# Two-directional state-space scan in a mixer kernel: step sizes in the exponents, decays added ahead of the scores, token-major inner sum, norm factors in the output weights, state chain by head

## The chip, the cores and the metric

One NeuronCore of one Trainium2 chip runs the whole program: both layers of the trunk, all 768 tokens. The metric is the device time of one execution in microseconds; the median of several executions is compared. Every time below is in microseconds unless it is marked ns. Engines are written as in the profile: PE (TensorE), DVE (VectorE), ACT (ScalarE), POOL (GpSimd) and SP (SyncE, whose queue issues most transfers).

## The reference

A trunk of two layers over 512 latent tokens and 256 context tokens (width 1024). Each layer has one input projection whose columns feed two groups of heads: a gated depthwise convolution with LayerNorm, and a state-space scan in both directions. Their outputs are concatenated, multiplied by `w_out` and added to the tokens; a mixture of experts (MoE) follows. The change touches the scan and the norm behind it:

```python
SSD_HEADDIM = 64; SSD_HEADS = 8; SSD_GROUPS = 2; SSD_STATE = 128; SSD_CHUNK = 128

def ssd_chunked(xs, dt, a, bm, cm, h0):      # one direction
    a_cum = jnp.cumsum((dt * a).reshape(b, nc, SSD_CHUNK, nh), axis=2)
    xdt = (xs * dt[..., None]).reshape(b, nc, SSD_CHUNK, nh, hp)
    causal = jnp.tril(jnp.ones((SSD_CHUNK, SSD_CHUNK), dtype=bool))
    seg = a_cum[:, :, :, None, :] - a_cum[:, :, None, :, :]
    decay_ls = jnp.exp(jnp.where(causal[None, None, :, :, None], seg, -jnp.inf))
    scores = jnp.einsum("bclhn,bcshn->bclsh", cc, bc) * decay_ls
    y_diag = jnp.einsum("bclsh,bcshp->bclhp", scores, xdt)
    decay_to_end = jnp.exp(a_cum[:, :, -1:, :] - a_cum)
    chunk_states = jnp.einsum("bclh,bclhn,bclhp->bchpn", decay_to_end, bc, xdt)
    chunk_decay = jnp.exp(a_cum[:, :, -1, :])
    # h_prev: scan over chunks of  h * chunk_decay + chunk_states
    y_off = jnp.einsum("bclhn,bchpn,bclh->bclhp", cc, h_prev, jnp.exp(a_cum))
    return (y_diag + y_off).reshape(b, l, nh, hp)

def mixer_output(...):
    y = y_f + y_b + p["d_skip"][:, None] * xs
    ssd_out = rms_norm(y.reshape(b, l, D_SSD) * jax.nn.silu(z), p["ssd_norm_g"])
    return jnp.concatenate([conv_out, ssd_out], axis=-1) @ p["w_out"]
```

## The kernel before

The tokens are cut into chunks of 128: chunks 0 to 3 are latent, 4 and 5 context. Layer 0 scans all six; layer 1, the last, needs only the latent four, but forms the states of all. A chunk lies with its tokens on the 128 partitions, so a 128x512 tile is one chunk of all eight heads. The arithmetic of this part is fp32. `xs` and `zs` (the scan's input and its gate) are the two halves of the tile `bigA`.

The mixer of a layer runs through four stages that overlap:

1. The input projection. `xbc_tile` (line 814) makes the columns of x, B and C, one tile of 128 columns at a time, with a short convolution as five DVE instructions (lines 830 and 832); `decays` (line 792) makes the step sizes' cumulated decays, writes their transposed sums to DRAM as `cumd`, and keeps the factors `ex` and the negative sums `ncum`.
2. The states. For each chunk POOL multiplies `xs` by both directions' factors (line 936), PE turns B (line 939), DVE copies it (line 941), PE forms two 128x512 states (line 947), ACT and DVE copy them from PSUM into `wraw` or `tab` (line 949). Then the chain: four steps in each direction, a state times its decay plus the next state (line 959 on DVE, line 960 on DVE or, for the backward direction, on POOL), through a temporary of the pool `Y`. The last columns of C, the chunks of z and the LayerNorm of the convolution (`ln_steps`, line 881, with the square root at line 364 on POOL and the multiply at line 906 on DVE) run beside it.
3. The scan, chunk by chunk. `prep` (line 971) reads a chunk's row of `cumd` to all partitions for each direction (line 975), masks it on POOL (line 977) and takes eight exponentials on ACT (line 980), into one of two pairs of decay buffers `E`. `scores` (line 982) forms C times B on PE (line 986) and C times the incoming states (line 993), multiplies both directions' decays by the scores on DVE (line 997), scales `xs` by both directions' step sizes on POOL (line 998) and starts `Y` with the skip term (line 1000) and the states' part (lines 1003 and 1004). `inside` (line 1007) sums both directions over the chunk with 32 matmuls whose result stands channel by token (line 1013), copies it from PSUM (line 1016), turns it back with four transposes (line 1019), adds it and multiplies by z (lines 1020 and 1021), and takes the RMS norm with the gain `sng` (lines 1023 and 1025). `turn_y` (line 1027) turns `Y` again for the output projection (lines 1030, 1033, 1034).
4. The output projection. One unit is two chunks times 256 columns: 48 matmuls (lines 491 to 493). Layer 0 has 12 units, layer 1 has 8. The first ones stand between chunks of the scan, the others follow it; `out_weights` (line 1042) loads `w_out` and splits it in two parts (lines 1059 and 1060).

The loop over chunks writes `prep` of chunk c+1 ahead of `inside` of chunk c; the decays of chunk c+2 use the buffers of chunk c. Within that, the order of instructions on each engine is set by a scheduler that simulates a timeline when the program is built; an engine then works strictly in that order. Pools bound it: eight buffers for `t4`, three for `Y`, two for `t2` and `wp`, two PSUM buffers each for `sm`, `tp` and `mm`. The MoE behind each mixer streams its weights into the buffers that the mixer frees.

```python
for c in order:
    Ys[c] = scores(c)
    if c < order[-1]:
        prep(c + 1)
    if units:
        out_proj(*units.pop(0))
    if c:
        turn_y(c - 1, Ys[c - 1])
        residual(c - 1)
    inside(c, Ys[c])
```

## Time and profile before

| what | us |
|---|---|
| median of three executions (1306.15 to 1311.55) | 1311.16 |
| the profiled execution, its own time | 1300.17 |
| its span | 1298.5 |
| busy in it: PE / DVE / ACT / POOL | 1100.1 / 784.1 / 550.7 / 570.7 |
| scan and end of output projection, layer 0 | about 331 to 461 |
| scan and end of output projection, layer 1 | about 958 to 1052 |

The profile is of one execution, 10.99 us below the median. PE is busy in 85% of the span, but the share of each stage differs, so the stages are read one by one: a view with busy times by stretch, then the timeline of the engines in it. In a timeline a group of like instructions in a row is one line with its count; the bracket at its end is the idle time ahead of it on its engine and what released it. In the view by stretch each engine has its busy time and the number of its instructions, then come the granted TensorE clock (1.00 is full speed), the busy share of the DMA engines and GB/s.

### The profile page before, as it was taken

To read this page: it belongs to the slowest core of one execution; us is meant where nothing else is said; L and a number is where in the kernel's file an instruction comes from. 1 tells how busy PE (TensorE), PEld (TensorE's weight loads), DVE (VectorE), ACT (ScalarE), POOL (GpSimd) and SP (SyncE) were. 2 spreads that over 40 slices of the span, in tenths; PEclk is the share of its full clock that TensorE was granted. 3 is DMA by queue.
4 is the path that set the end of the run, shared out by engine and by line. 5 is a ranking of instruction groups with operands and counts; after the bars stand their busy time and mean duration, and the time that the engine had idled before them with its cause. 6 is when DMAs were issued, how large, how long until landed. Compare 5 with 4: busy or idle time off the path is not lost. (4 is left out here: it accounts for less than half of the span.)

```text
span 1298.5 us, 20274 instructions
## 1 busy us (share of the span) xinstructions
PE 1100.1 (85%) x7595; PEld 915.6 (71%) x7595; DVE 784.1 (60%) x1199; ACT 550.7 (42%) x976; POOL 570.7 (44%) x445
## 2 busy tenths in 40 slices
...
DMA packets 113810, 261.18 MB, mean 201 GB/s; under 512 B 16033, under 2 KB 53519, under 8 KB 108589
## 3 DMA queue, kind: packets, MB, share of 16 engines
...
q8 instruction: 61, 1.00, 0.3%
...
## 5 line engine op out<-in xcount | busy, mean ns | idle before, releaser
L474 POOL TENSOR_TENSOR t<-wp,t 128x1024 fp32r<-128x1024 f32 (+1 forms) x36 | 99.2, 2760 | 192.2 <-ACT t L473 187.1
L491 PE MATMUL mm<-t,HL 128*128 128x256 f32 (+1 forms) x448 | 133.3, 298 | 8.0 <-DVE acc L906 4.0
L493 PE MATMUL mm<-t,HL 128*128 128x256 f32 (+1 forms) x448 | 130.4, 291 | 1.1 <-DVE HL L1034 1.1
L492 PE MATMUL mm<-t,HL 128*128 128x256 f32 (+1 forms) x448 | 130.1, 290 | 0.0
L1461 POOL DMA_INDIRECT acc_d<-t,idx x38 | 70.5, 1856 | 77.7 <-ACT t L1456 24.9
L1376 POOL TENSOR_TENSOR C<-raw,wraw 128x1024 fp32r<-128x1024 f32 x28 | 78.4, 2850 | 58.9 <-PE sm L493 39.6
L491 PEld LDWEIGHTS mm<-t,HL 128*128 128x128 f32 x448 | 87.9, 196 | 17.6 <-issue 6.5
L493 PEld LDWEIGHTS mm<-t,HL 128*128 128x128 f32 x448 | 87.6, 196 | 5.4 <-issue 3.7
L492 PEld LDWEIGHTS mm<-t,HL 128*128 128x128 f32 x448 | 87.9, 196 | 4.9 <-issue 4.8
L832 DVE SCALAR_TENSOR_TENSOR t<-t,pcol,t 128x772 f32<-128x772 f32 (+1 forms) x64 | 87.8, 1372 | 2.1
L492 PE MATMUL sm<-C,t 128*128 128x256 f32 (+8 forms) x304 | 85.7, 282 | 3.9 <-DVE C L1376 3.9
L491 PE MATMUL mm<-HL,t 128*128 128x512 f32 (+1 forms) x224 | 85.0, 380 | 2.8 <-ACT HL L385 1.6
L364 POOL TENSOR_TENSOR rstd<-ms,mhalf 128x1 f32<-128x1 f32 (+3 forms) x29 | 23.0, 796 | 143.9 <-DVE ms L362 143.9
L492 PE MATMUL mm<-HL,t 128*128 128x512 f32 (+1 forms) x224 | 82.8, 370 | 0.0
L493 PE MATMUL mm<-HL,t 128*128 128x512 f32 (+1 forms) x224 | 82.4, 368 | 0.0
L1375 ACT CAST wraw<-raw 128x1024 fp32r<-128x1024 f32 x64 | 66.0, 1048 | 35.8 <-DMA raw<-in_w_down_dram 18.7
L493 PE MATMUL sm<-HL,t 128*128 128x256 f32 (+8 forms) x272 | 77.3, 284 | 1.9 <-DVE t L1406 1.9
L492 PE MATMUL sm<-HL,t 128*128 128x256 f32 (+8 forms) x272 | 76.7, 282 | 2.2 <-DVE HL L1376 2.2
L491 PE MATMUL sm<-HL,t 128*128 128x256 f32 (+8 forms) x272 | 78.3, 288 | 0.1
L473 ACT CAST t<-wp 128x1024 fp32r<-128x1024 f32 (+1 forms) x40 | 41.9, 1056 | 82.8 <-PE mm L492 63.9
L1384 POOL DMA_INDIRECT t<-h2d,idx x38 | 52.8, 1390 | 52.6 <-PE sm L1360 16.6
L1376 POOL TENSOR_TENSOR HL<-raw,HL 128x1024 fp32r<-128x1024 f32 x24 | 61.2, 2603 | 19.9 <-ACT HL L1375 14.8
...
## 6 DMA issues: line engine op xcount, KB each, us to landing
...
raw<-in_w_gate_dram SPq DMA_DIRECT2D x60, 512.0 KB
raw<-in_w_up_dram SPq DMA_DIRECT2D x60, 512.0 KB
raw<-in_w_down_dram SPq DMA_DIRECT2D x60, 512.0 KB
wp<-in_w_in_dram SPq DMA_DIRECT2D x40, 512.0 KB
wp<-in_w_out_dram SPq DMA_DIRECT2D x16, 512.0 KB
...
v<-cumd SPq DMA_DIRECT2D x15, 512.0 KB
```

What stands on the lines that cost most here:

```text
L364: G.tensor_tensor(r[:, :n], ms[:, :n], mhalf[:, :n], op=OP.pow)
L473: S.copy(hi, t)
L474: eng.tensor_sub(lo, t, hi)
L491: T.matmul(dst, lh, rh, start=(k == 0), stop=False)
L492: T.matmul(dst, lh, rl, start=False, stop=False)
L493: T.matmul(dst, ll, rh, start=False, stop=(k == K8 - 1))
L832: V.scalar_tensor_tensor(xa[:, :n], xpt[:, tap:tap + n], col, xa[:, :n], op0=OP.mult, op1=OP.add)
L1375: highs.append(S.copy(hi, r))
L1376: eng.tensor_sub(lo, r, hi)
L1384: gathered.append(G.indirect_dma_start(out=xg[:n], out_offset=None, in_=h2d, in_offset=bass.IndirectOffsetOnAxis(ap=icol[:n], axis=0)))
L1461: G.indirect_dma_start(out=acc_d, out_offset=bass.IndirectOffsetOnAxis(ap=icol[:n], axis=0), in_=y[:n], in_offset=None, compute_op=OP.add)
```

## The change

- **Step sizes in the exponents.** The scores need the decay times dt. The kernel takes ln(dt), floored at 1e-37, adds it to `ncum` and uses the sum `ldt` as the bias of the exponentials. Two DVE instructions and one ACT instruction a layer are new in `decays`; the POOL multiply of `xs` by the step sizes (line 998) goes.
- **Both directions added ahead of the scores.** A POOL addition of 128x1024 joins the two directions' exponentials in `prep`; one DVE multiply by the scores is left of two. The second buffer of a pair is free after the addition.
- **Inner sum token major.** Eight matmuls with the decays of a head as stationary operand and 64 columns of `xs` moving give the result token by channel; the 32 matmuls, the copy and the four transposes go.
- **Norm.** The gain goes into the second half of the output weights, one DVE multiply of 128x1024 for each of four column blocks a layer, from columns of the parameter tile; the load of `sng` becomes a small load at the start. The RMS factor goes into a diagonal matrix (a DVE instruction of 128x128), and `turn_y` multiplies `Y` by it instead of by the identity; line 1025 goes.
- **Chain by head.** Each of the eight steps is eight DVE instructions of 128x64 that multiply and add in one, 64 a layer, in place of eight multiplies on DVE and eight additions on DVE and POOL. The temporary goes.

```diff
--- before.py
+++ after.py
@@ -195,7 +195,7 @@
     dsk = const.tile([P, 2, 8], F32, name="dsk")
     rb = const.tile([P, 2, 2, 20], F32, name="rb")
     wr = const.tile([P, 2, K8, 32], F32, name="wr")
-    pcol = const.tile([P, 120], F32, name="pcol")
+    pcol = const.tile([P, 128], F32, name="pcol")
     cwcol = [const.tile([P, 124], F32, name=f"cwcol{l}") for l in range(2)]
     av = const.tile([P, 2, 16], F32, name="av")
     block0, capv = [const.tile([P, 2, 16], F32, name=n) for n in ("block0", "capv")]
@@ -207,10 +207,11 @@
 
     def params():
         rows = main.tile([P, 4, P], F32, name="ad", bufs=3)
-        prow, cwrow = rows[:120, 0], rows[:124, 1:3]
+        prow, cwrow = rows[:128, 0], rows[:124, 1:3]
         for off, n, src in ((0, 8, conv_b), (8, 8, conv_ln_g), (16, 8, conv_ln_b), (24, 16, ssd_conv_b)):
             nc.sync.dma_start(out=prow[off:off + n, :], in_=src.rearrange("l (k p) -> (l k) p", p=P))
         nc.sync.dma_start(out=prow[40:120, :], in_=ssd_conv_w.rearrange("l t (k p) -> (l t k) p", p=P))
+        nc.sync.dma_start(out=prow[120:128, :], in_=ssd_norm_g.rearrange("l (k p) -> (l k) p", p=P))
         nc.sync.dma_start(out=cwrow, in_=conv_w.rearrange("l t (k p) -> (t k) l p", p=P))
         nc.sync.dma_start(out=dtb.rearrange("p l e -> p (l e)"), in_=bcast(dt_bias, 0, [[0, P], [1, 32]]))
         nc.sync.dma_start(out=alog.rearrange("p l e -> p (l e)"), in_=bcast(a_log, 0, [[0, P], [1, 32]]))
@@ -533,7 +534,7 @@
         vB, vC = [t.rearrange("p a b -> p (a b)").rearrange("p (j t) -> p j t", j=2) for t in (vB, vC)]
         for n, b in (("Y", 3), ("t2", 2)):
             mixp.tile([P, 512], F32, name=n, bufs=b)
-        dtr, dts, dA, ncum = [mixp.tile([P, 2, 6, 8], F32, name=n) for n in ("dtr", "dts", "dA", "ncum")]
+        dtr, dts, dA, ncum, ldt = [mixp.tile([P, 2, 6, 8], F32, name=n) for n in ("dtr", "dts", "dA", "ncum", "ldt")]
         ex = mixp.tile([P, 3, 2, 6, 8], F32, name="ex")
         BT = mixp.tile([P, 2, NT], F32, name="BT")
         CT = mixp.tile([P, 2, NT], F32, name="CT")
@@ -798,6 +799,9 @@
             S.activation(ex.rearrange("p q d c h -> p (q d c h)"), ps[:, :288], AF.Exp)
             V.tensor_mul(ex[:, 1], ex[:, 1], dts)
             V.tensor_scalar(f96(ncum), ps[:, 288:384], -1.0, None, op0=OP.mult)
+            V.tensor_scalar(ldt, dts, 1e-37, None, op0=OP.max)
+            S.activation(ldt, ldt, AF.Ln)
+            V.tensor_add(ldt, ldt, ncum)
             pt = tp_tile()
             T.transpose(pt[0:96, 0:P], f96(ncum), ident)
             cumT = main.tile([P, 512], F32, name="ad", bufs=3)
@@ -920,8 +924,6 @@
             for i in range(7):
                 nc.sync.dma_start(out=acc_d[i * P:(i + 1) * P, :], in_=z)
 
-        sng = main.tile([P, 512], F32, name="ad", bufs=3)
-        nc.sync.dma_start(out=sng, in_=bcast(ssd_norm_g, l * 512, [[0, P], [1, 512]]))
         rooms["held"], rooms["next"] = False, 0
         Sb, Sa, Sc = [wraw_tile([P, 4, 512], F32) for _ in range(3)]
         St = {4: [Sa[:, 0], Sa[:, 1]], 5: [Sa[:, 2], Sa[:, 3]], 1: [Sb[:, 0], Sb[:, 1]],
@@ -955,9 +957,10 @@
         for i in range(1, 5):
             for d in range(2):
                 c0, c1 = chain[d][i - 1], chain[d][i]
-                t = mixp.tile([P, 512], F32, name="Y", bufs=3)
-                V.tensor_mul(hview(t), hview(St[c0][d]), hbc(ex[:, 2], d, c1, 64))
-                (G if d else V).tensor_add(St[c1][d], St[c1][d], t)
+                for h in range(NH):
+                    hs = slice(64 * h, 64 * h + 64)
+                    V.scalar_tensor_tensor(St[c1][d][:, hs], St[c0][d][:, hs], ex[:, 2, d, c1, h:h + 1], St[c1][d][:, hs],
+                                           op0=OP.mult, op1=OP.add)
         ln_fill()
         af(1)
         fill(1)
@@ -977,7 +980,9 @@
                 G.affine_select(out=e, in_=e, pattern=[[0, NH], [(1, -1)[d], P]],
                                 compare_op=OP.is_ge, fill=-1e30, base=0, channel_multiplier=(-1, 1)[d])
                 for h in range(NH):
-                    S.activation(e[:, h, :], e[:, h, :], AF.Exp, bias=ncum[:, d, c, h:h + 1])
+                    S.activation(e[:, h, :], e[:, h, :], AF.Exp, bias=ldt[:, d, c, h:h + 1])
+            e = E[c % 2]
+            G.tensor_add(e[0], e[0], e[1])
 
         def scores(c):
 
@@ -992,10 +997,8 @@
                 for g in range(2):
                     T.matmul(pf[:, d * 512 + g * 256:d * 512 + (g + 1) * 256], CT[:, g, c * P:(c + 1) * P],
                              H[:, g * 256:(g + 1) * 256], start=True, stop=True)
-            for d in range(2):
-                e = E[c % 2][d].rearrange("p (g h) q -> p g h q", g=2)
-                V.tensor_mul(e, e, pq[:, :256].rearrange("p (g q) -> p g q", g=2)[:, :, None, :].to_broadcast([P, 2, 4, P]))
-            G.tensor_mul(v4(xdt), hview(xs[:, c, :])[:, None].to_broadcast([P, 2, NH, 64]), both(dts, c, 64))
+            e = E[c % 2][0].rearrange("p (g h) q -> p g h q", g=2)
+            V.tensor_mul(e, e, pq[:, :256].rearrange("p (g q) -> p g q", g=2)[:, :, None, :].to_broadcast([P, 2, 4, P]))
             Y = mixp.tile([P, 512], F32, name="Y", bufs=3)
             G.tensor_mul(hview(Y), hview(xs[:, c, :]), dsk[:, l, :, None].to_broadcast([P, NH, 64]))
             for i, d in enumerate(dirs):
@@ -1006,28 +1009,23 @@
 
         def inside(c, Y):
 
-            pyT = sm_tile()
-            for h in range(0, NH, 2):
-                for d in range(2):
-                    for j in range(2):
-                        T.matmul(pyT[64 * j:64 * j + 64, h * 64:h * 64 + P], xdt[:, d, (h + j) * 64:(h + j + 1) * 64],
-                                 E[c % 2][d][:, h + j, :], start=(d == 0), stop=(d == 1))
-            yT = t2_tile()
-            (V.tensor_copy if last else S.copy)(yT, pyT)
-            py = tp_tile()
-            for f in range(4):
-                T.transpose(py[:, f * P:(f + 1) * P], yT[:, f * P:(f + 1) * P], ident)
+            py = sm_tile()
+            for h in range(NH):
+                hs = slice(64 * h, 64 * h + 64)
+                T.matmul(py[:, hs], E[c % 2][0][:, h, :], xs[:, c, hs], start=True, stop=True)
             V.tensor_add(Y, Y, py)
             V.tensor_mul(Y, Y, zs[:, c, :])
             ss = sml.tile([P, 8], F32, name="ss")
-            S.activation(yT, Y, AF.Square, accum_out=ss[:, 0:1])
+            S.activation(t2_tile(), Y, AF.Square, accum_out=ss[:, 0:1])
             r = rstd_of(ss, 1, 512.0, RMS_EPS)
-            V.scalar_tensor_tensor(Y, Y, r[:, 0:1], sng, op0=OP.mult, op1=OP.mult)
-
-        def turn_y(c, Y):
+            dg = main.tile([P, P], F32, name="diag", bufs=2)
+            V.tensor_scalar(dg, ident, r[:, 0:1], None, op0=OP.mult)
+            return Y, dg
+
+        def turn_y(c, Y, dg):
             pt = tp_tile()
             for f in range(4):
-                T.transpose(pt[:, f * P:(f + 1) * P], Y[:, f * P:(f + 1) * P], ident)
+                T.matmul(pt[:, f * P:(f + 1) * P], Y[:, f * P:(f + 1) * P], dg, start=True, stop=True)
             p3 = pt.rearrange("p (f t) -> p f t", f=4)
             ks = slice(4, 8)
             S.copy(mh(ks, c * P, (c + 1) * P), p3)
@@ -1048,6 +1046,8 @@
                 raw.append(main.tile([P, 4, 256], F32, name="wp", bufs=2))
                 nc.sync.dma_start(out=raw[h], in_=w_out[l][512 * h:512 * h + 512, 256 * n4:256 * n4 + 256]
                                   .rearrange("(k p) n -> p k n", p=P))
+
+            V.tensor_mul(raw[1], raw[1], pcol[:, 120 + 4 * l:124 + 4 * l, None].to_broadcast([P, 4, 256]))
             for h in range(2):
                 if n4 == 2:
                     hi.append(t2[:, h])
@@ -1092,7 +1092,6 @@
         prep(0)
         split_conv(range(4))
         acc2 = mixp.tile([P, 3, 2, 512], F32, name="acc")
-        xdt = acc2[:, 0]
         ws, units, Ys = {}, [], {}
         for c in order:
             Ys[c] = scores(c)
@@ -1104,14 +1103,14 @@
             if units:
                 out_proj(*units.pop(0))
             if c:
-                turn_y(c - 1, Ys[c - 1])
+                turn_y(c - 1, *Ys[c - 1])
                 residual(c - 1)
-            inside(c, Ys[c])
+            Ys[c] = inside(c, Ys[c])
             if c < 2 or c == 4:
                 ws[min(c, 2)] = out_weights(min(c, 2))
             if c and c % 2 == 0:
                 units += [(n4, ws[n4], c - 2) for n4 in range(2)]
-        turn_y(c, Ys[c])
+        turn_y(c, *Ys[c])
         residual(c)
         for n4 in range(2, 4):
             if n4 not in ws:
```

The scheduler also puts other work in another place. On POOL in layer 0, the three skip terms `Y<-bigA,dsk` stood behind the selects and among the chain's additions:

```order
L977 AFFINE_SELECT v<-v 128x1024
L960 TENSOR_TENSOR wraw<-wraw,Y 128x512
L1000 TENSOR_TENSOR Y<-bigA,dsk 128x512 x2
L960 TENSOR_TENSOR wraw<-wraw,Y 128x512
L1000 TENSOR_TENSOR Y<-bigA,dsk 128x512
L1090 TENSOR_TENSOR HL_2628<-acc,HL_2626 128x512 x2
```

Now they stand ahead of the six multiplies of `xs` that the states begin with (line 936 before, 938 now), as they do in layer 1:

```order
L980 AFFINE_SELECT tab<-tab 128x1024
L899 TENSOR_TENSOR v<-v 128x768 x3
L1003 TENSOR_TENSOR Y<-bigA,dsk 128x512 x3
L938 TENSOR_TENSOR t_2199<-bigA,ex 128x1024
L938 TENSOR_TENSOR t_2214<-bigA,ex 128x1024
```

What moved are the three `Y` instructions, ahead of what the states wait for. On DVE in the same stage of layer 0, before, copies of B from PSUM (`t<-tp`), copies of states (`wraw<-sm`, `tab<-sm`) and the first steps of the chain (lines 959 and 960):

```order
L941 COPY t_2216<-tp 128x256
L959 TENSOR_TENSOR Y<-wraw,ex 128x512
L949 COPY wraw<-sm 128x512
L941 COPY t_2231<-tp 128x256
L960 TENSOR_TENSOR wraw<-wraw,Y 128x512
L949 COPY wraw<-sm 128x512
L941 COPY t_2242<-tp 128x256
L959 TENSOR_TENSOR Y<-wraw,ex 128x512 x2
L941 COPY t_2253<-tp 128x256
L960 TENSOR_TENSOR tab<-tab,Y 128x512
```

and the same place now, with the steps of 64 columns at line 962:

```order
L962 SCALAR_TENSOR_TENSOR wraw<-wraw,ex 128x64 x6
L951 COPY wraw<-sm 128x512
L943 COPY t_2245<-tp 128x256
L962 SCALAR_TENSOR_TENSOR wraw<-wraw,ex 128x64 x2
L943 COPY t_2256<-tp 128x256
L962 SCALAR_TENSOR_TENSOR wraw<-wraw,ex 128x64 x8
L962 SCALAR_TENSOR_TENSOR tab<-wraw,ex,tab 128x64 x7
L951 COPY tab<-sm 128x512
L943 COPY t_2271<-tp 128x256
L962 SCALAR_TENSOR_TENSOR tab<-wraw,ex,tab 128x64
L962 SCALAR_TENSOR_TENSOR wraw<-tab,ex,wraw 128x64 x7
L951 COPY wraw<-sm 128x512
```

Between the copies there now stand 31 short instructions instead of five long ones; 48 of the 64 are ahead of the last copy of a state. On SP's queue in the scan of layer 0, where `v<-cumd` and `tab<-cumd` are the reads for the decays, before:

```order
L975 DMA v<-cumd_1567 128x1024 x3
L1049 DMA wp<-in_w_out_dram 128x4x256 x5
L355 DMA acc<-ada_1059 128x2x512 x2
L1049 DMA wp<-in_w_out_dram 128x4x256
L975 DMA v<-cumd_1567 128x1024 x3
L1065 DMA bigA<-in_x_dram 128x2x512
L975 DMA tab<-cumd_1567 128x1024
```

and now:

```order
L978 DMA v<-cumd_1569 128x1024 x3
L1047 DMA wp<-in_w_out_dram 128x4x256
L978 DMA v<-cumd_1569 128x1024
L978 DMA tab<-cumd_1569 128x1024
L1047 DMA wp<-in_w_out_dram 128x4x256 x2
L356 DMA acc<-ada_1061 128x2x512 x2
L978 DMA v<-cumd_1569 128x1024
L1047 DMA wp<-in_w_out_dram 128x4x256
L978 DMA v<-cumd_1569 128x1024
```

One read for chunk 2 and one for chunk 3 moved ahead of loads of output weights, since the buffer of the second direction is free earlier.

## Rows read from the trace of the kernel before

**Rows 1.** Busy time by stretch, layer 0's and layer 1's state, scan and projection stages.

```profile
285.00:330.00 45.00, 36.29 (x220) 32.88 (x220) 38.16 (x35) 23.53 (x46) 30.84 (x23) 0.85 0.28 84
330.00:390.00 60.00, 44.38 (x395) 38.56 (x394) 45.39 (x53) 33.61 (x90) 46.49 (x33) 0.94 0.50 164
390.00:460.00 70.00, 70.00 (x573) 65.31 (x574) 34.42 (x62) 19.28 (x50) 9.38 (x8) 1.00 0.25 78
...
930.00:958.00 28.00, 24.06 (x164) 18.27 (x162) 25.14 (x23) 20.48 (x39) 20.08 (x15) 0.94 0.73 262
958.00:1020.00 62.00, 50.57 (x411) 42.02 (x407) 46.64 (x57) 24.89 (x56) 37.33 (x25) 0.94 0.66 226
1020.00:1040.00 20.00, 20.00 (x161) 18.68 (x162) 9.22 (x17) 4.87 (x15) 1.71 (x2) 1.00 0.03 10
```

**Rows 2.** Timeline of PE in layer 0's scan, chunks 0 to 2.

```profile
340.00 1.97 PE L1013 MATMUL sm<-v,acc 128*64 128x128 f32 x32 [0.81 <-POOL acc L998]
...
341.89 0.71 PE L986 MATMUL sm<-CT,BT 128*128 128x128 f32 x4
...
342.70 0.66 PE L1019 MATMUL tp<-ident,t 128*128 128x128 f32 x4
...
356.82 1.12 PE L1030 MATMUL tp<-ident,Y 128*128 128x128 f32 x4 [7.66 <-DVE Y L1025]
...
358.72 2.91 PE L1013 MATMUL sm<-v,acc 128*64 128x128 f32 x32
```

**Rows 3.** Timeline of the other engines between `inside` of chunks 0 and 2.

```profile
341.78 5.15 SPq L975 DMA_DIRECT2D v<-cumd  x3
...
349.16 1.28 ACT L980 ACT_TABLE_LOAD   x1 [6.51 <-DMA v<-cumd]
...
350.45 2.44 ACT L980 ACTIVATE v<-v,ncum 128x128 f32<-128x128 f32 x8
...
351.43 1.90 POOL L998 TENSOR_TENSOR acc<-bigA,dts 128x1024 f32<-128x1024 f32 x1
...
352.99 1.22 DVE L997 TENSOR_TENSOR v<-v,sm 128x1024 f32<-128x1024 f32 x1 [5.60 <-ACT v L980]
...
353.28 1.09 POOL L977 TENSOR_SCALAR_AFFINE_SELECT v<-v 128x1024 f32<-128x1024 f32 x1
...
354.96 1.81 DVE L1025 SCALAR_TENSOR_TENSOR Y<-Y,rstd,ad 128x512 f32<-128x512 f32 x1
```

**Rows 4.** Timeline of PE in layer 1's scan, chunks 0 and 2.

```profile
968.48 1.74 PE L1013 MATMUL sm<-v,acc 128*64 128x128 f32 x26
...
988.00 1.75 PE L1013 MATMUL sm<-v,acc 128*64 128x128 f32 x28 [1.39 <-DVE v L997]
```

**Rows 5.** Timeline of POOL and DVE in layer 0's state stage.

```profile
274.25 12.55 POOL L936 TENSOR_TENSOR t<-bigA,ex 128x1024 f32<-128x1024 f32 x6 [1.23 <-ACT bigA L850]
...
277.99 2.42 DVE L959 TENSOR_TENSOR Y<-wraw,ex 128x512 f32<-128x512 f32 x1 [1.69 <-ACT wraw L949]
...
286.75 2.79 POOL L474 TENSOR_TENSOR t<-wp,t 128x1024 fp32r<-128x1024 f32 x1
...
296.14 0.69 DVE L949 COPY wraw<-sm 128x512 f32<-128x512 f32 x1 [2.59 <-PE sm L947]
...
298.38 0.69 DVE L959 TENSOR_TENSOR Y<-wraw,ex 128x512 f32<-128x512 f32 x1
...
298.99 0.68 DVE L959 TENSOR_TENSOR Y<-tab,ex 128x512 f32<-128x512 f32 x1
...
304.51 3.06 POOL L474 TENSOR_TENSOR t<-wp,t 128x1024 fp32r<-128x1024 f32 x1
...
312.81 3.34 DVE L906 TENSOR_TENSOR acc<-acc,mm 128x3072 f32<-128x3072 f32 x1
```

**Rows 6.** One line's forms with least, median and longest ns, first and last start.

```profile
L790 DVE SCALAR_TENSOR_TENSOR acc<-v,cwcol,acc x56: 269/479/2560, 103.6 to 789.1; 128x64 f32<-128x64 f32 x8, 128x128 f32<-128x128 f32 x8, 128x192 f32<-128x192 f32 x8, 128x256 f32<-128x256 f32 x8
```

**Rows 7.** Timeline of ACT around the step sizes of layer 0.

```profile
202.85 0.59 ACT L821 COPY t<-mm 128x512 f32<-128x512 f32 x1 [10.86 <-PE mm L493]
```

## The prediction

> **What bounds the kernel now.** I read the busy times by stretch first, then the timeline of the engines in the scan. In layer 0's scan (330 to 390) no engine is full: PE is busy 44.4 of 60 us, DVE 45.4, POOL 46.5, ACT 33.6. Behind it, from 390 to 460, PE is busy all the time [rows 1]. So the mixer ends when the scan is through and PE has done what is left of the output projection. PE's idle time in the scan is 60 - 44.38 = 15.6 us, and 7.66 of it is one wait, for the normed `Y` of chunk 0 [rows 2]. Behind that stands a loop over the decay buffers. Chunk 2 reuses chunk 0's pair: its reads are issued at 341.78, when `inside` of chunk 0 has used the pair up, and ACT's exponentials wait for them until 349.16. DVE waits 5.60 us for those exponentials with its score multiply, and the norm of chunk 0 stands behind that multiply on DVE [rows 3]. From `inside` of chunk 0 to that of chunk 2 the loop takes 358.72 - 340.00 = 18.7 us [rows 2]. In layer 1 it takes 988.00 - 968.48 = 19.5 us [rows 4], and PE is idle 62 - 50.57 = 11.4 us from 958 to 1020 [rows 1]. In the stage before, where the states are made, DVE is busy 38.2 of 45 us in layer 0 and 25.1 of 28 in layer 1, the highest share of all [rows 1]. That stage decides when the scan begins.
>
> **The change, part by part.** *Matmuls of the inner sum.* A chunk loses 32 matmuls of 1.97 us and four transposes of 0.66 [rows 2], 2.63 together. The eight new ones have a 128x128 stationary operand and 64 moving columns; the nearest row is four of 128 by 128 in 0.71 [rows 2], so eight cost between 0.71 (half the columns) and 1.42. I take the upper end, as the operand to be loaded is as large as in that row. `turn_y` as a true matmul costs that row's 0.71 instead of 0.66. That leaves 1.2 to 1.9 saved a chunk, and I take 1.25. Only what lies where PE is otherwise full counts: chunks 2 to 5 of layer 0, behind the wait, 4 x 1.25 = 5.0, and chunks 2 and 3 of layer 1, 2.5.
>
> *The loop.* The new route from `inside` of chunk 0 to that of chunk 2 is: `inside` 1.4, the read 349.16 - 341.78 = 7.4, the select 1.09, one direction's exponentials 2.44, POOL's addition as the nearest POOL row of 128x1024, 1.90, and one score multiply 1.22 [rows 3]. That is 15.45 us against 18.7, 3.3 less. The other direction's read and exponentials, and ACT's table load of 1.28 with them, can go ahead, since the addition frees that buffer. If the read also lands in half the time, as half of its bytes have gone before, the loop is 7.0 shorter. I take the middle, 5.2, in layer 0. In layer 1 the same route gives 19.5 - 15.45 = 4.1 to 7.8, and I take the lower end: the DMA engines are busier there, 0.66 against 0.50 [rows 1].
>
> *DVE and POOL in the scan.* POOL's multiply of 1.90 goes and an addition of about 1.90 comes, so POOL is even. DVE loses a score multiply of 1.22 and a norm of 1.81 a chunk [rows 3] and gets a 128x128 multiply that should be a quarter of the 512 columns' 0.69 [rows 5] and the start-up, 0.3: some 2.7 less a chunk, 16 in layer 0. The four multiplies of the output weights cost between 1.22 each [rows 3] and 1.22 + (2.42 - 0.69) = 2.95 when POOL is in the way [rows 5], 5 to 12 us a layer. DVE has room for these: nothing on the path. The cover is gone if one of them waits at the head of DVE for its weights; then the next score multiply waits too.
>
> *Logarithm.* ACT's logarithm and its table load (1.28 [rows 3]) fall into an idle time of 10.86 us [rows 7]: nothing. In all the order has eight table loads more, five of them in layer 1 about the start of the scan, 5 x 1.28 = 6.4 us on an engine that is idle 28 - 20.48 = 7.5 us there [rows 1]. Between nothing and 6.4 I take 1 us for the path, since most of it fits.
>
> A rule of the Trainium skill differs here: "ScalarE: Activation LUTs", section "What ACT_TABLE_LOAD costs", has about 1380 ns of draining beside a load of 1283 ns. The first exponential stands at 350.45, directly behind the load that began at 349.16 [rows 3], so the trace shows no drain after it. By the page's figure the 1 us would be about twice that, an estimate, and the time 1304.
>
> *The chain and the state stage.* This is where I expect a loss. The three skip terms go ahead of the six multiplies that the states start with, on POOL: 3 x about 1.0 (half of the 1.90 for 1024 columns [rows 3]), so these end 3 us later than 274.25 + 12.55 = 286.8, and with POOL's next instruction (2.79) POOL is busy to about 292.6 [rows 5]. As long as POOL runs back to back, a chain multiply that takes 0.69 alone takes 2.42 [rows 5]: it gets through when a POOL instruction ends. A step of 64 columns would take 0.2 alone: the least of that shape is 0.269 [rows 6], less the 0.08 by which neighbours overlap (the multiply at 298.38 takes 0.69, the next begins 0.61 later [rows 5]). Beside POOL it should get through at the same rate as the large ones, one for each POOL instruction. Ten POOL instructions let some ten steps through. Of the 48 steps ahead of the last state copy 38 are left at 292.6: 38 x 0.2 + 1.4 for two copies = 9.0, so that copy comes at about 302 instead of 296.14 [rows 5], 6 us late. PE waits for it, but has 45 - 36.29 = 8.7 us of idle time in this stretch [rows 1]; if a third of it lies behind that copy, 4 us is left. DVE itself is to be no later than that at the LayerNorm's multiply (312.81 [rows 5]), as the chain's large instructions between are gone. I take 4 us late in each layer. The bounds are 0, when the lost POOL additions and large multiplies pay for it, and 9, when nothing absorbs the three skip terms and the six.
>
> The Trainium skill's page "SBUF — State Buffer", section "Who interferes with whom", has a rule that speaks against this part: a VectorE instruction with two SBUF inputs and a GpSimd instruction that reads SBUF exclude each other for a whole instruction, and whichever begins second is blocked. The trace agrees: 2.42 against 0.69 [rows 5]. Without the rule 64 steps of 0.2 would be 12.8 us, less than the old chain's eight multiplies and four additions took under contention, and the term would be nothing or a gain: 1295. With it pushed to the end, it is the third rival.
>
> **Sum.** Layer 0: -5.2 (loop) - 5.0 (PE) + 4.0 (late) = -6.2. Layer 1: -4.0 - 2.5 + 4.0 + 1.0 = -1.5. Together -7.7 on the profiled execution's 1300.17, so 1292.5. That execution lies 10.99 below the median 1311.16, so I forecast 1311.2 - 7.7 = 1303.5, in round numbers 1303. The MoE's weights come into buffers that the mixer frees, so I let the gain pass to the end.
>
> **The rivals.** *More gain.* The state stage is not late, the reads land in half the time and the matmuls cost the lower bound: layer 0 by 7.0 + 4 x 1.9 = 14.6, but POOL's 46.5 busy us of 60 [rows 1] stop that at 13.5; layer 1 by 7.8 + 3.8 = 11.6, less 1: 24 in all, 1287. For it: 7.66 us in one wait that the new order takes apart. Against it: POOL has as much to do as before.
>
> *No change.* The change doesn't shorten the loop, because POOL's addition queues behind other POOL work and stands between exponentials and scores. Only PE's 7.5 us are left, and a stage that is late by 8 with 1 of tables eats them: +1.5, 1313. For it: POOL is the busiest engine of layer 0's scan [rows 1]. Against it: a second direction's exponentials no longer wait for the read.
>
> *Slower.* The chain's short steps stay caught between POOL instructions also behind 292.6. Two weight splits like that at 304.51 (3.06) [rows 5] and three selects of 1.09 [rows 3] then hold one step each instead of one large multiply, 2 x 3.06 + 3 x 1.09 = 9.4 us; with the 4 us the stage is late by some 13.5 in each layer, and PE waits for states behind it. Against 9.2 + 7.5 = 16.7 of gains that is 27 + 1: +11.3, 1322. It decides from 11 us of lateness in each layer. For it: one multiply took 2.42 instead of 0.69. Against it: in layer 0's later part multiplies ran at 0.69 each [rows 5], when POOL had little to do.
>
> **How the numbers follow.** A measurement of this kernel tells about 0.5% from no change, 6.6 us: below 1304.6 is faster, above 1317.7 slower. The forecast's case has 45%, spread over 1297 to 1309; some three fifths of it lie below 1304.6, so 27% go to faster and 18% to the same. The larger gain has 20%. No change has 17%, of which 13% stay within the bound and 4% are slower. The slower case has 18%. Together: faster 0.47, same 0.31, slower 0.22. For 8 in 10 the range reaches into both outer cases: 1286 to 1321.
>
> **What would show it.** Right: PE's long wait ahead of `turn_y` of chunk 0 shrinks below 4 us, `inside` of chunk 2 follows that of chunk 0 by 12 to 15.5 us, eight matmuls take 0.7 to 1.4, the last copy of a state is some 6 us late against the first of the six POOL multiplies of before, and steps of 64 columns show two lengths, about 0.27 and about 2. Wrong: the steps are short throughout, or long also behind the POOL block; the wait for the decays moves to POOL's addition; a multiply of output weights stands at the head of DVE and waits for its load; or layer 1's scan is held by table loads.

## The result and the profile after

The changed kernel takes 1329.88 us (median of 4 runs, 1327.19 to 1332.50), the kernel before 1310.91 us beside it (4 runs). The ratio is 1.0145, with a 95% interval of 1.0112 to 1.0178: slower by about 1.5%, where 1303 was forecast. The profiled execution has a span of 1325.4 us against 1298.5, and a mean granted clock of 0.918 against 0.933.

The busy times by stretch of the changed kernel answer to [rows 1]; the columns are the same (busy us of PE, PEld, DVE, ACT and POOL, granted clock, DMA share, GB/s):

```profile
285.00:330.00 45.00, 27.70 (x157) 24.68 (x156) 44.96 (x86) 20.16 (x40) 26.05 (x19) 0.85 0.32 105
330.00:390.00 60.00, 46.46 (x312) 43.42 (x311) 42.78 (x53) 37.80 (x94) 39.70 (x30) 0.86 0.40 132
390.00:460.00 70.00, 63.94 (x492) 60.78 (x491) 36.05 (x48) 12.90 (x32) 14.18 (x9) 0.93 0.27 76
```

Two things stand out. In the stage of the states of layer 0 (285 to 330) DVE is full, 44.96 of 45 us where it was 38.2, and PE has fallen from 36.29 to 27.70. And from 390 to 460, where PE had been busy all the time, it now idles 6 us.

**Where the 27 us of span went.** I cut the program at four points that every version has: the start of POOL's block for the states (of the skip terms, where these stand directly ahead of it), and the start of the last eviction of the output projection (the DVE instruction that reads its last PSUM tile), in each layer. Before, layer 0's stretch took 185.5 us and layer 1's 140.9; after, 201.9 and 145.0. What lies between the layers took 450.1 and 450.4. So layer 0 lost 16.4 us, layer 1 4.2, the rest (the start 1.0, behind layer 1 5.1) 6.4 in all. By the medians of the timed runs the loss is 19 us, not 27, since the profiled execution of before lies 10.99 below its median. These two stretches are used for every experiment below. Each comes from one profiled execution, and each edit also lets the scheduler place other work differently, so a few us between two stretches decide nothing by themselves; the ratios come from the timed runs.

**The stage of the states.** The timeline of DVE in layer 0 answers to [rows 5] (start, duration, engine, line, operation, out<-in, count, and in brackets idle time and what ended it; line 962 is a step of the chain, 951 a state's copy), and POOL's below it:

```profile
282.26 0.69 DVE L951 COPY wraw<-sm 128x512 f32<-128x512 f32 x1 [4.68 <-PE sm L949]
...
283.88 8.36 DVE L962 SCALAR_TENSOR_TENSOR wraw<-wraw,ex 128x64 f32<-128x64 f32 x6 [0.60 <-ACT wraw L951]
292.16 0.68 DVE L951 COPY wraw<-sm 128x512 f32<-128x512 f32 x1
...
293.81 1.64 DVE L962 SCALAR_TENSOR_TENSOR wraw<-wraw,ex 128x64 f32<-128x64 f32 x8
...
297.87 3.68 DVE L962 SCALAR_TENSOR_TENSOR wraw<-tab,ex,wraw 128x64 f32<-128x64 f32 x7
...
305.30 3.83 DVE L962 SCALAR_TENSOR_TENSOR wraw<-wraw,ex 128x64 f32<-128x64 f32 x8
...
309.98 0.68 DVE L951 COPY wraw<-sm 128x512 f32<-128x512 f32 x1
...
275.27 3.05 POOL L1003 TENSOR_TENSOR Y<-bigA,dsk 128x512 f32<-128x512 f32 x3 [0.99 <-ACT bigA L854]
278.27 11.19 POOL L938 TENSOR_TENSOR t<-bigA,ex 128x1024 f32<-128x1024 f32 x6
289.42 2.34 POOL L475 TENSOR_TENSOR t<-wp,t 128x1024 fp32r<-128x1024 f32 x1
...
298.79 2.48 POOL L475 TENSOR_TENSOR t<-wp,t 128x1024 fp32r<-128x1024 f32 x1 [6.92 <-ACT t L474]
...
306.34 2.51 POOL L475 TENSOR_TENSOR t<-wp,t 128x1024 fp32r<-128x1024 f32 x1 [5.07 <-PE sm L949]
```

Read the two engines side by side. The first step begins at 283.88, when the first states are there; six steps then took 8.36 us. A closer window shows how, two steps and the two POOL multiplies beside them:

```profile
285.75 3.79 DVE L962 SCALAR_TENSOR_TENSOR wraw<-wraw,ex 128x64 f32<-128x64 f32 x2
285.70 3.76 POOL L938 TENSOR_TENSOR t<-bigA,ex 128x1024 f32<-128x1024 f32 x2
```

Each step lasts as long as the POOL instruction that began just before it. Four of the six went so, beside three multiplies and a weight split; the last two took 0.2 each, once POOL had ended at 291.76. Copies stood behind them until 292.16. While POOL paused, eight steps took 1.64, 0.2 each. Each time POOL came back with a weight split (298.79, 306.34), it held one step for 2.5 us, so that seven took 3.68 and eight 3.83. The last copy of a state comes at 309.98 instead of 296.14 [rows 5], which is 34.7 us from the start of the block instead of 21.9: 12.8 us late.

The finished states are not late: the chain ends at 316.64, 41.4 us from the start of the block, where it ended at 319.70, after 45.4. Late is what stands behind the steps on DVE and what needs it. PE's rows in this stage, first of before, then of after, layer 0 and layer 1 (`sm<-t,t` makes the states, `sm<-ones,v` sums for the LayerNorm of the convolution, `mm<-ident,rstd` uses the result):

```profile
295.94 1.40 PE L900 MATMUL sm<-ones,v 128*128 128x1 f32 x12
...
928.70 1.03 PE L900 MATMUL sm<-ones,v 128*128 128x1 f32 x8
...
293.31 2.04 PE L949 MATMUL sm<-t,t 128*128 128x256 f32 x4 [8.10 <-DVE t L943]
...
307.35 1.39 PE L904 MATMUL sm<-ones,v 128*128 128x1 f32 x12
315.42 2.93 PE L909 MATMUL mm<-ident,rstd 128*128 128x128 f32 x12 [5.51 <-POOL rstd L365]
...
955.96 0.95 PE L904 MATMUL sm<-ones,v 128*128 128x1 f32 x8
```

PE waits 8.10 us for a copy of B that stands behind the six steps, and 5.51 for the LayerNorm's power. Counted from the block's start, the LayerNorm's sums are 10.4 us late in layer 0 and 9.6 in layer 1, and the first inner sum of the scan (345.62 in layer 0, 995.60 in layer 1) is 4.6 and 9.4 late.

**The scan.** DVE's waits from 330 to 480 in layer 0, grouped (engine, what waits, what it waits for: total us, times, longest), and under them the rows of the timeline in which they stand:

```profile
DVE wp L1050 <- DMA wp<-in_w_out_dram: 17.4, 3, 8.6
```

```profile
337.99 1.22 DVE L1050 TENSOR_TENSOR wp<-wp,pcol 128x1024 f32<-128x1024 f32 x1 [2.92 <-DMA wp<-in_w_out_dram]
...
360.59 2.13 DVE L1050 TENSOR_TENSOR wp<-wp,pcol 128x1024 f32<-128x1024 f32 x1 [5.83 <-DMA wp<-in_w_out_dram]
...
363.24 1.11 DVE L1022 TENSOR_SCALAR diag<-ident,rstd 128x128 f32<-128x128 f32 x1
...
413.22 1.22 DVE L1050 TENSOR_TENSOR wp<-wp,pcol 128x1024 f32<-128x1024 f32 x1 [8.64 <-DMA wp<-in_w_out_dram]
...
364.41 2.08 PE L1028 MATMUL tp<-diag,Y 128*128 128x128 f32 x8 [6.05 <-DVE diag L1022]
...
414.69 2.08 PE L1028 MATMUL tp<-diag,Y 128*128 128x128 f32 x8 [5.38 <-DVE diag L1022]
```

The multiply of the output weights by the gain (line 1050) stands at the head of DVE and waits for its load. The diagonal of the norm (1022, at 363.24 and 414.36) stands behind it, and PE waits 6.05 and 5.38 us for that diagonal. The wait of 7.66 us for the normed `Y` [rows 2] has become two.

### The profile page after: what moved, and what is told of

The parts are those of the page before. It is cut to its first block, busy times and chain, and to the rows that moved or that the text cites. A ratio compares the mean times of both kernels' runs of the same rounds, so it can differ in the third digit from the quotient of the medians.

```text
span 1325.4 us, 20030 instructions
## 1 busy us (share of the span) xinstructions
PE 1106.0 (83%) x7435; PEld 926.3 (70%) x7435; DVE 789.7 (60%) x1301; ACT 560.3 (42%) x980; POOL 556.1 (42%) x437
## 5 line engine op out<-in xcount | busy, mean ns | idle before, releaser
L475 POOL TENSOR_TENSOR t<-wp,t 128x1024 fp32r<-128x1024 f32 (+1 forms) x36 | 96.0, 2671 | 208.6 <-ACT t L474 202.1
L492 PEld LDWEIGHTS mm<-t,HL 128*128 128x128 f32 x448 | 89.7, 200 | 14.1 <-issue 7.4
L1460 POOL DMA_INDIRECT acc_d<-t,idx x38 | 67.8, 1784 | 63.3 <-DMA acc_d<-t,idx 20.5
L494 PEld LDWEIGHTS mm<-t,HL 128*128 128x128 f32 x448 | 89.0, 199 | 6.7 <-issue 5.3
L493 PEld LDWEIGHTS mm<-t,HL 128*128 128x128 f32 x448 | 89.6, 200 | 1.8 <-issue 1.7
L365 POOL TENSOR_TENSOR rstd<-ms,mhalf 128x1 f32<-128x1 f32 (+3 forms) x29 | 23.7, 819 | 149.9 <-DVE ms L363 125.4
L1383 POOL DMA_INDIRECT t<-h2d,idx x38 | 55.3, 1455 | 59.5 <-DMA acc_d<-t,idx 18.4
```

What stands on the lines that cost most here:

```text
L365: G.tensor_tensor(r[:, :n], ms[:, :n], mhalf[:, :n], op=OP.pow)
L475: eng.tensor_sub(lo, t, hi)
L492: T.matmul(dst, lh, rh, start=(k == 0), stop=False)
L493: T.matmul(dst, lh, rl, start=False, stop=False)
L494: T.matmul(dst, ll, rh, start=False, stop=(k == K8 - 1))
L1383: gathered.append(G.indirect_dma_start(out=xg[:n], out_offset=None, in_=h2d, in_offset=bass.IndirectOffsetOnAxis(ap=icol[:n], axis=0)))
```

## Experiments

Theories at the start: (a) the chain's short steps, with two operands in SBUF, get through one per POOL instruction; (b) the multiply of the output weights holds DVE; against both, (c) that the new scan itself (step sizes in the exponents, the addition, the token-major sum) is what costs, and (d) that the skip terms ahead of the states' block do.

All stretches in one table, in us (layer 0, layer 1). "Last state" is counted from the block's start in layer 0: the start of the last copy of a state out of PSUM or, where the chain itself reads PSUM (e5, e6, e9, e12, e14, e16), of its last eight steps. In the second kind these eight end the chain; in the first it goes on behind the copy (to 45.4 in before, 41.4 in after):

| version | last state | layer 0 | layer 1 | ratio to before |
|---|---|---|---|---|
| before | 21.9 | 185.5 | 140.9 | 1 |
| after | 34.7 | 201.9 | 145.0 | 1.0145 |
| e1: after, old chain | – | 193.3 | 143.0 | 1.0091 |
| e2: after, old norm | 34.7 | 191.3 | 143.8 | 1.0048 |
| e3: after, old chain and norm | 22.0 | 185.2 | 132.7 | 0.9919 |
| e4: before, new chain | 33.9 | 192.7 | 157.6 | 1.0131 |
| e5: after, chain adds from PSUM | 29.7 | 178.9 | 150.5 | 0.9975 |
| e6: e5, old norm | 29.7 | 178.9 | 142.5 | 0.9993 |
| e9: PSUM chain in layer 0, old in 1, old norm | 29.7 | 176.7 | 132.7 | 0.9926 |
| e12: before, PSUM chain in layer 0 | 28.1 | 185.1 | 148.1 | 1.0043 |
| e10: e3, channel-major sum | – | 187.5 | 137.3 | 0.9985 |
| e8: e3, gain in the weights | – | 190.1 | 136.6 | 0.9975 |
| e11: after, gain on POOL | – | 191.0 | 144.9 | 1.0081 |
| e13: after, gain on ACT | 34.7 | 185.0 | 144.2 | 1.0024 |
| e14: PSUM chain in layer 0, old in 1, gain on ACT | 29.7 | 176.8 | 140.2 | 0.9907 |
| e15: after, skip terms late | 30.0 | 199.0 | 152.6 | 1.0181 |
| e16: e9, skip terms late | 23.4 | 171.5 | 132.1 | 0.9836 |
| e17: e14, skip terms late | – | 179.0 | 142.2 | 1.0003 |
| e18: e12, skip terms late | – | 183.4 | 148.8 | 1.0039 |

### Undoing parts: e1 to e4

e1 puts the old chain back; e2 the old norm (the gain and the factor applied to `Y` on DVE, transposes by the identity); e3 both. e4 puts the new chain alone into the kernel before.

```diff
 # e1, and in e3; e4 is the same lines turned round in the kernel before
-                for h in range(NH):
-                    hs = slice(64 * h, 64 * h + 64)
-                    V.scalar_tensor_tensor(St[c1][d][:, hs], St[c0][d][:, hs], ...)
+                t = mixp.tile([P, 512], F32, name="Y", bufs=3)
+                V.tensor_mul(hview(t), hview(St[c0][d]), hbc(ex[:, 2], d, c1, 64))
+                (G if d else V).tensor_add(St[c1][d], St[c1][d], t)
 # e2, and in e3
-            V.tensor_scalar(dg, ident, r[:, 0:1], None, op0=OP.mult)
+            V.scalar_tensor_tensor(Y, Y, r[:, 0:1], sng, op0=OP.mult, op1=OP.mult)
-                T.matmul(pt[...], Y[...], dg, start=True, stop=True)
+                T.transpose(pt[...], Y[...], ident)
-            V.tensor_mul(raw[1], raw[1], pcol[...])
```

> The changed kernel with the chain of states as before: eight multiplies of 128x512 on DVE through a temporary, additions on DVE and POOL. Changed kernel: 1329.9; before: 1310.9; in the changed kernel's trace six steps of 64 columns took 8.36 us beside POOL's multiplies and a state copy stood behind them, the last state copy came 13.8 us later than before, and layer 0's mixer ended 17.4 later. Theory A (the chain's short steps, caught one for each POOL instruction, hold back the state copies, and with the three skip terms ahead make the stage late): about 1316, two thirds of the loss back; the last state copy of layer 0 again near 296 to 298. Theory B (the output weights' multiply waits at the head of DVE for its load and holds back the scan): 1327 to 1330, hardly better. Theory C (the new scores and inner sum are slower themselves): 1327 to 1330.

> The changed kernel with the norm as before: gain and RMS factor multiplied into Y on DVE, transposes by the identity, no multiply of the output weights. Theory A (chain): 1325 to 1329, the state stage as late as in the changed kernel. Theory B (weights' multiply: DVE waited 17.4 us in three waits for their loads in layer 0's part, the longest 8.6): about 1317, and no DVE wait for output weights; from inside of chunk 2 to the end of the mixer no further loss. Theory C: 1329.

> The changed kernel with both chain and norm as before; what is left of the change is the step sizes in the exponents, the addition ahead of the scores and the token-major inner sum. Theories A and B together: 1306 to 1311, at the kernel before or a little better, since POOL is even, DVE has less to do and the matmuls are at most 0.7 us a chunk less. Theory C: 1322 or more, the loss sits in what is left.

> The kernel before with only the chain by head, 64 steps of 64 columns a layer. Theory A: about 1322 to 1325, ten or more slower than before, with the same late state copies as in the changed kernel. Theories B and C: 1309 to 1313, no change.

Measured: e1 1317.50 us, 1.0091 [1.0061, 1.0121]; e2 1316.44, 1.0048 [1.0015, 1.0080]; e3 1298.14, 0.9919 [0.9879, 0.9959]; e4 1325.41, 1.0131 [1.0081, 1.0181]. e1, e2 and e4 came out within 2 us of what the theories had led me to expect, e3 some 8 us better. Without chain and norm the rest of the change is a gain, so (c) falls. In the two stretches together e3 takes 317.9 us, 8.5 less than before (326.4); the new chain on top of it costs 17.2 (e2, 335.1), the new norm 18.4 (e1, 336.3), both 29.0 (after, 346.9). The two overlap: undoing one alone gives back 10.6 or 11.8. e4 has the same picture as after: six steps in 8.25 us beside POOL, the last state 33.9 us from the block's start. So the lateness comes with the chain, whatever the scan. Alone in the kernel before, the chain costs nearly as much as the whole change (1.0131 against 1.0145), most of it in layer 1 (157.6 against 140.9).

In e3 all of the gain is in layer 1 (132.7 against 140.9); layer 0 gains 0.3. But the wait for the normed `Y` is gone there. PE in e3, the rows of the timeline for `inside` of chunks 0 and 2 and for the transposes of chunk 0:

```profile
346.49 1.89 PE L1016 MATMUL sm<-bigA,v 128*128 128x64 f32 x16
...
361.97 0.66 PE L1028 MATMUL tp<-ident,Y 128*128 128x128 f32 x4 [0.69 <-DVE Y L1022]
365.20 3.65 PE L1016 MATMUL sm<-bigA,v 128*128 128x64 f32 x16 [2.57 <-issue]
```

0.69 us is left of 7.66, while the loop from `inside` of chunk 0 to that of chunk 2 takes 365.20 - 346.49 = 18.7 us, as long as before.

### Is it the two operands in SBUF? e5, e6, e9, e12

e5 keeps the chain by head, but makes the states in the chain's order and takes the added operand out of PSUM, where the matmul leaves it; the copy of the state goes. Nothing of POOL's work is changed. e6 is e5 with the old norm; e9 has this chain in layer 0 alone, the old one in layer 1, and the old norm; e12 is the kernel before with this chain in layer 0.

```diff
-                (V.tensor_copy if d and not last else S.copy)(St[c][d], ps)
...
-                    V.scalar_tensor_tensor(St[c1][d][:, hs], St[c0][d][:, hs], ex[:, 2, d, c1, h:h + 1], St[c1][d][:, hs],
+                V.scalar_tensor_tensor(St[c][d][:, hs], St[before_of[d][c]][d][:, hs], ex[:, 2, d, c, h:h + 1], ps[:, hs],
                                        op0=OP.mult, op1=OP.add)
```

> The changed kernel, its chain still by head in steps of 64 columns, but the new state is taken straight from PSUM as the added operand: 64 steps a layer with one SBUF tensor input instead of two, and no copies of those states. Nothing is left out. The skip terms still stand ahead of the six multiplies. Theory A (lock): steps take about 0.2 each also beside POOL's multiplies, the first eight under 2 us instead of six in 8.36, and the last state of layer 0 is there within 25 us of the block's start (34.7 in the changed kernel, 21.9 before); time some 6 to 10 below the changed kernel's, 1318 to 1322 by the first session's times. Rival (it is the number of short instructions ahead of the copies, whatever they read): steps as slow or the states no earlier, no gain.

> The same chain from PSUM, with the norm as before: left of the change are step sizes, addition, token-major sum and this chain. Theory A: at or below the version with old chain and old norm (0.992 of the kernel before), since 64 steps without the lock replace copies, multiplies and additions: 0.985 to 0.995. Rival: 1.005, as with the new chain and the old norm.

> Old norm; the chain from PSUM in layer 0 only, the old chain in layer 1; step sizes, addition and token-major sum as in the change. From the stretches of the runs so far: with the chain from PSUM layer 0's states, scan and projection took 178.9 us (before 185.6), and with the old chain and old norm layer 1's took 132.8 (before 140.9). If the two layers' stretches add, it is 14 to 15 us under the kernel before, 0.987 to 0.991. Rival (what one stretch gains the transfers behind it give back, as the run with the chain from PSUM in both layers stood at 0.999): 0.994 to 1.000.

> The kernel before with the chain from PSUM in layer 0 only. Theory A (lock): the last state of layer 0 is there as early as in the other runs with this chain, about 25 us after the first of POOL's multiplies with the skip terms counted, and the time is 0.993 to 0.999, as the stage ends earlier. If the skip terms' three microseconds and the short steps eat it: 1.000 to 1.004.

The timeline of DVE in e5, same place, and POOL's block beside it:

```profile
284.17 1.62 DVE L958 SCALAR_TENSOR_TENSOR wraw<-wraw,ex,sm 128x64 f32<-128x64 f32 x8 [0.24 <-PE sm L951]
...
278.26 11.20 POOL L941 TENSOR_TENSOR t<-bigA,ex 128x1024 f32<-128x1024 f32 x6
```

Eight steps of the same shape take 1.62 us beside the same POOL block: in layer 0 all 64 take 265 to 280 ns. With both operands in SBUF they took 269 to 2497. That settles (a) for the length of the steps. The gain in time is that of the whole edit, in which the copies of these states go too and the states are made in another order. The Trainium skill's page "SBUF — State Buffer", section "Who interferes with whom", says that a VectorE instruction with at most one SBUF input, outside the two-port modes, does not contend with GpSimd; the trace agrees (265 to 280 ns).

e5 has 1304.61 us, 0.9975 [0.9947, 1.0002]; e6 1306.60, 0.9993 [0.9965, 1.0022]; e9 1295.01, 0.9926 [0.9899, 0.9953]. e5 is some 13 us better than expected, e6 and e9 miss their ranges (0.985 to 0.995, 0.987 to 0.991) on the slow side. Layer 0's stretch falls by 23 us (201.9 to 178.9), and with that chain the norm costs layer 0 nothing more (e6 178.9): DVE still has the multiply of the output weights in e5, but waits only 3.1 us for their loads from 330 to 480. In layer 1 the same code is a loss against the old chain (142.5 in e6, 132.7 in e9 and e3). Why is open: I have no run that takes it apart. The trace of e6 shows PE waiting 4.6 us there for the LayerNorm's power, a wait that e9 does not have. The 8.0 us by which e5 is longer than e6 in layer 1 do not show in the timed runs (0.9975 and 0.9993).

e12: 1311.27 us, 1.0043 [1.0015, 1.0070]. On the kernel before the PSUM chain gains 0.4 us in layer 0, and layer 1, whose code it does not touch, takes 148.1 instead of 140.9. The first inner sum of the scan comes 3.4 us earlier from the block's start than in before. With the new scan the same chain brings it 7.8 us earlier and layer 0 8.5 (e3 to e9: 185.2 to 176.7). So the earlier state stage paid in layer 0 only together with the new scan; what gives it back in e12, and the rise in layer 1, are open.

### The norm: e7, e8, e11, e13

e7 and e8 start from e3. e7 multiplies by the diagonal but leaves the gain out; e8 puts the gain into the weights, applies the factor to `Y` on DVE and keeps the transposes. e11 and e13 start from the changed kernel and move the multiply of the output weights to POOL and to ACT.

```diff
 # e11
-            V.tensor_mul(raw[1], raw[1], pcol[...])
+            G.tensor_mul(raw[1], raw[1], pcol[...])
 # e13
-            V.tensor_mul(raw[1], raw[1], pcol[...])
+            for k in range(4):
+                S.activation(raw[1][:, k, :], raw[1][:, k, :], AF.Copy, scale=pcol[:, 120 + 4*l + k:121 + 4*l + k])
 # e8, against e3
-            V.scalar_tensor_tensor(Y, Y, r[:, 0:1], sng, op0=OP.mult, op1=OP.mult)
+            V.tensor_scalar(Y, Y, r[:, 0:1], None, op0=OP.mult)
+            V.tensor_mul(raw[1], raw[1], pcol[...])
```

> Old chain; the norm by the diagonal matrix as in the change, but without the multiply of the output weights, so the gain is left out of the result. Against old chain with old norm (0.992) and old chain with the whole new norm (1.009). Theory B (the weights' multiply waits for its load at the head of DVE): 0.990 to 0.997, most of the loss gone. Rival (the diagonal matmul costs: eight matmul rows a chunk instead of four, a 128x128 multiply that takes POOL's lock): 1.005 to 1.010.

> Old chain; the gain in the output weights as in the change, but the RMS factor multiplied into Y on DVE and transposes by the identity. Nothing is left out. Theory B: 1.003 to 1.010, with DVE waits for the output weights' load of 6 us or more, and PE waits in the projection behind it. Rival (diagonal): 0.990 to 0.996.

> The changed kernel, the multiply of the output weights by the gain on POOL instead of DVE; nothing else. The changed kernel stands at 1.0145. Theory B (the multiply waits for the weights' load at the head of DVE, 17.4 us in three waits in layer 0's scan): the DVE waits go; if POOL's queue has room, 1.004 to 1.009. Rival (the wait only changes the engine: POOL's masks, additions and square roots stand behind it now): 1.012 to 1.020.

> The changed kernel, the gain multiplied into the output weights by four ACT instructions a column block instead of one on DVE; ACT waits for that load there anyhow, for its own copy of the weights. Nothing is left out. The changed kernel stands at 1.0145, with the multiply on POOL at 1.008. If waiting at the head of DVE is the norm's cost: 1.002 to 1.007, about what the new chain with the old norm took (1.005), and no DVE wait for output weights. If multiply and diagonal matmul cost by themselves: 1.009 to 1.015.

e7 leaves the gain out, so other data reach the MoE, and what lies between the layers takes 493.2 us instead of 450; its 1336.26 us, 1.0193 [1.0140, 1.0246], therefore says nothing about the norm, and the run was badly chosen. Its stretches can be compared only as far as the mixer goes: 184.1 and 136.7, so the diagonal alone costs layer 0 nothing and layer 1 4.0. e8: 1305.28, 0.9975 [0.9943, 1.0008], 190.1 and 136.6: the weights' multiply alone costs 4.9 and 3.9 against e3, and the ratio lies between the ranges of the two theories. Together (e1) they cost 8.1 and 10.3, more than the sum of the two (3.8 and 7.9): a likely reason, not tested by itself, is that with both it is the diagonal that stands behind the waiting multiply.

e13: 1312.37, 1.0024 [0.9989, 1.0060]; e11: 1320.18, 1.0081 [1.0050, 1.0113]. The wait itself, from 330 to 480, in e13 and in e11:

```profile
ACT wp L1051 <- DMA wp<-in_w_out_dram: 10.8, 2, 7.4
```

```profile
POOL wp L1050 <- DMA wp<-in_w_out_dram: 10.2, 2, 10.0
...
DVE diag L1022 <- POOL rstd L365: 7.8, 2, 7.5
```

The loads are still waited for; what changes is who stands behind the wait. On ACT nothing urgent does: PE's waits for the diagonal fall from 11.4 us to 0.7, and layer 0 from 201.9 to 185.0: 16.9 us, about the 17.4 that DVE had waited. On POOL the norm's power (`rstd`) stands behind it, the diagonal waits 7.5 us for that, and PE 4.4 for the diagonal. This settles (b), for layer 0. In layer 1 DVE had waited 1.5 us for these loads, and the stretch hardly changes (145.0 to 144.2). The wait hangs on the state stage as well: with the multiply on DVE it is 17.4 us in after, 11.5 with the old chain (e1) and 3.1 with the chain from PSUM (e5).

### The inner sum: e10

e10 is e3 with the sum in the old form (channel by token, a copy, four transposes), but with one matmul a head, since both directions are already added.

```diff
-                T.matmul(py[:, hs], E[c % 2][0][:, h, :], xs[:, c, hs], start=True, stop=True)
+                    T.matmul(pyT[64 * j:64 * j + 64, ...], xs[:, c, ...], E[c % 2][0][:, h + j, :], start=True, stop=True)
...
+                T.transpose(py[:, f * P:(f + 1) * P], yT[:, f * P:(f + 1) * P], ident)
```

> Old chain, old norm, step sizes in the exponents and the addition ahead of the scores, but the inner sum channel by token with copy and transposes as before (half as many matmuls as before, since there is one direction). Against the same with the token-major sum (0.992). If the token-major sum is what gained: 0.997 to 1.003. If the addition and the loss of one score multiply gained: 0.990 to 0.995.

1306.41 us, 0.9985 [0.9958, 1.0011]. The stretches sum to 324.8, against 317.9 in e3 and 326.4 before: step sizes in the exponents and the addition are worth 1.6 us, less than one execution can show; the token-major sum is worth 6.9, and the timed runs agree (0.9985 against 0.9919).

### The skip terms, and the versions that could win: e14 to e18

e14 is the chain of e9 with the gain on ACT in place of the old norm. e15 holds the three skip terms back until the last state is there: a one-column copy into each `Y` that reads the last state makes POOL's instruction depend on it. e16 is e9 with that, e17 is e14 with that, e18 is e12 with that.

```diff
+        for _ in range(3):
+            late = mixp.tile([P, 512], F32, name="Y", bufs=3)
+            V.tensor_copy(late[:, 0:1], St[2][0][:, 0:1])
         ln_fill()
```

> The chain from PSUM in layer 0, the old chain in layer 1, the whole new norm with its gain multiplied on ACT, the rest as in the change. The same with the old norm took 0.9926. If the norm costs only by its wait: 0.988 to 0.995. If the diagonal matmul and the multiply cost by themselves: 0.998 to 1.004.

> The changed kernel, with three tiny DVE copies a layer that hold the buffers of Y until the chain's forward end, so that the skip terms stand behind POOL's multiplies of the states again. By the prediction's step these are 3 us a layer ahead of all that follows: last state copy of layer 0 some 3 us earlier against the start of POOL's block, time 1.010 to 1.012. Rival (the block is bound by POOL and the short steps alone, and the skip terms then stand in the way later): unchanged, 1.013 to 1.016.

> The best version so far (0.9926: old norm, chain from PSUM in layer 0) with the skip terms held back behind POOL's multiplies. If these three microseconds are on the path: 0.989 to 0.992. If not: 0.992 to 0.995.

> The best version so far (0.984: step sizes, addition, token-major sum, chain from PSUM in layer 0, skip terms held back, old norm) with the new norm instead, its gain multiplied on ACT. If the norm without its wait is neutral, as 0.9907 against 0.9926 said: 0.980 to 0.987. If the diagonal matmul costs: 0.989 to 0.995.

> The kernel before with the chain from PSUM in layer 0 and the skip terms held back: scores of both directions, POOL's scaling of xs, channel-major sum and norm as before. If the scan's parts are what gains (0.992 on old chain and norm): 0.993 to 1.001. If the chain and the held-back skip terms are all: 0.983 to 0.988.

e14: 1294.71, 0.9907 [0.9870, 0.9944]. e15: 1331.72, 1.0181 [1.0122, 1.0239]: the last state is 4.7 us earlier, layer 0 is 2.9 shorter, layer 1 7.6 longer, and nothing is gained (both ranges expected were lower); theory (d) falls as the reason for the loss. On the version whose other waits are gone, the same edit is worth something: **e16 takes 1284.19 us, 0.9836 [0.9801, 0.9871], faster than both kernels.** That is better than either range expected. Its last state comes 23.4 us from the block's start. Its busy times by stretch, to be set against those of after above and [rows 1]:

```profile
285.00:330.00 45.00, 36.50 (x238) 33.60 (x239) 34.18 (x81) 27.82 (x60) 27.50 (x23) 0.92 0.38 118
330.00:390.00 60.00, 52.05 (x361) 48.98 (x361) 47.84 (x58) 31.10 (x77) 45.78 (x32) 0.86 0.54 157
```

DVE is down to 34.18 of 45 us in the state stage, and PE is busy 36.50 us there and 52.05 in the scan, against 36.29 and 44.38 before. e16 keeps the new scan with its token-major sum, and the old norm; its chain by head reads the added operand from PSUM in layer 0, and layer 1 keeps the old chain.

e17 misses: 1307.47, 1.0003 [0.9978, 1.0028]. The new norm with its gain on ACT costs no time that the ratios tell where the skip terms come early (e9 and e14, 0.9926 and 0.9907, though layer 1's stretch is 7.5 us longer in e14) and 1.7% where they come late (e16 and e17). Layer 0 is 7.5 us longer there, layer 1 10.1. Order and buffers differ in many places between these two, and I have no run that singles one out: open. e18: 1314.54, 1.0039 [1.0003, 1.0075]: on the kernel before the two edits gain nothing, and the ratio is above either range expected. So the gain of e16 needs the new scan with them.

## Why the prediction was wrong

**The weights' multiply, priced at nothing.** This step and the next cost most, and they overlap; which of the two is the larger is not settled (undoing one alone gives 1.0048, e2, and 1.0091, e1, but the chain alone costs 1.0131, e4). The prediction named its cover ("The cover is gone if one of them waits at the head of DVE for its weights") and then took it as given. In layer 0 three of four waited, 17.4 us in all; moved to ACT, layer 0 was 16.9 us shorter. The loads have two buffers, so a later one is issued only when an earlier block has been split. The waits of SP's queue in layer 0 of after (from 300 to 420), and the last of these loads in its timeline:

```profile
SPq L1047 <- DVE t L1060: 18.2, 2, 11.3
```

```profile
398.31 0.53 SPq L1047 DMA_DIRECT2D wp<-in_w_out_dram  x1
```

That load is issued at 398.31, and its multiply begins at 413.22, the moment at which DVE's wait for it ends. So 14.9 us pass behind the issue: six other transfers of 512 KB had been issued from 394.22 on. How much of the waits is late issue and how much such a queue, no run separates. In the kernel before ACT's cast is the first to read these blocks, and no engine waits for a load of `wp` from 330 to 480. To ask for each of the four multiplies when its load lands and what stands behind it on DVE would have shown the loss.

**The state stage, 4 us late a layer.** The place was right, and so was the rate: steps take 0.2 us each without POOL (0.2 forecast), and beside it one gets through for each POOL instruction. The size was off. The prediction let ten steps through beside ten POOL instructions, but six of the ten were over before the first step could begin: four got through, and 44 were left, not 38. It let these run at 0.2 with two copies, 9.0 us; behind 291.76 it took 18.2, since two weight splits of POOL held a step each, and since copies, and the convolution's instructions of 0.6 to 1.0, stand among them. So the last copy of a state came 12.8 us late against 6. The wait that mattered was another than the one named: the prediction had DVE no later than 4 us at the LayerNorm's multiply, and from the block's start that multiply (322.02, 312.81 before [rows 5]) is 8.2 late. In layer 0 the first inner sum of the scan is 4.6 us late, close to the 4 forecast; as the parts behind it are other ones, that is luck. In layer 1 it is 9.4 late. The last copy of a state is only 4.6 late there; the LayerNorm's sums on PE, which followed the states directly in before, now stand behind 4.7 us of the projection's matmuls as well (951.22 to 955.96) and are 9.6 late. That is read from the trace; no run moves them by themselves. On e3 the new chain costs 6.1 us in layer 0 and 11.1 in layer 1 (e2), against 4.0 forecast for each. The rival that ends slower named steps held behind the POOL block and a threshold of 11 us in each layer: by the copies layer 0 passed it, by the first inner sum neither layer did.

**PE, 7.5 us saved.** The price came from a row whose count was misread. In the lines below each fp32 matmul leaves two rows, a transpose one. All rows of the new sum and the new `turn_y`, and of the old `turn_y` in the kernel before, grouped by form (busy us, mean ns):

```profile
L1015 PE MATMUL sm<-bigA,v 128*128 128x64 f32 x160 | 22.8, 304 | 5.3 <-DVE v L1001 5.3
L1028 PE MATMUL tp<-diag,Y 128*128 128x128 f32 x80 | 13.0, 311 | 11.5 <-DVE diag L1022 11.4
```

```profile
L1030 PE MATMUL tp<-ident,Y 128*128 128x128 f32 x40 | 6.8, 295 | 13.0 <-DVE Y L1025 13.0
```

Ten chunks of eight matmuls give 160 rows, ten of four products with the diagonal 80, ten of four transposes 40. The sum takes 1.89 us a chunk (16 rows), not 0.71 to 1.42, and `turn_y` 1.05 at full clock, not 0.71. A chunk saves 1.97 + 0.66 + 0.66 [rows 2] less 1.89 + 1.05, 0.35 us, not 1.25, so six chunks save 2.1 and not 7.5. The "four of 128 by 128 in 0.71" were two matmuls, and the 32 rows of line 1013, called 32 matmuls in the sections ahead, are 16 matmuls.

**The loop, 5.2 and 4.0 us shorter.** It is longer. From `inside` of chunk 0 to that of chunk 2 it takes 23.3 us in layer 0 (18.7 before [rows 2]) and 1019.27 - 995.60 = 23.7 in layer 1 (19.5 [rows 4]; the first four rows of chunk 2's 32 stand at 986.17 there, so from first row to first row it was 17.7). The rows of the loop in the timeline of after, engine by engine:

```profile
345.62 1.89 PE L1015 MATMUL sm<-bigA,v 128*128 128x64 f32 x16
...
368.93 3.46 PE L1015 MATMUL sm<-bigA,v 128*128 128x64 f32 x15 [2.45 <-DVE v L1001]
...
334.47 11.56 SPq L1047 DMA_DIRECT2D wp<-in_w_out_dram  x2
347.54 0.88 SPq L356 DMA_DIRECT2D acc<-ada  x2
348.51 0.42 SPq L978 DMA_DIRECT2D v<-cumd  x1
...
359.26 1.28 ACT L983 ACT_TABLE_LOAD   x1 [5.28 <-DMA v<-cumd]
360.55 2.44 ACT L983 ACTIVATE v<-v,ldt 128x128 f32<-128x128 f32 x8
...
363.10 1.17 POOL L980 TENSOR_SCALAR_AFFINE_SELECT v<-v 128x1024 f32<-128x1024 f32 x1
364.24 2.36 POOL L985 TENSOR_TENSOR v<-v 128x1024 f32<-128x1024 f32 x1
...
364.98 2.17 DVE L1017 TENSOR_TENSOR Y<-Y,bigA 128x512 f32<-128x512 f32 x1
...
367.67 1.20 DVE L1001 TENSOR_TENSOR v<-v,sm 128x1024 f32<-128x1024 f32 x1
```

The read is issued at 348.51, behind two loads of output weights and two of `ada`, and lands at 359.3: 10.8 us instead of 7.4, where I had reckoned with 7.4 or half of it. The table load is not ahead of the read but behind it; beside POOL's select of 1.09 its 1.28 adds 0.2. POOL's addition takes 2.36 instead of 1.90, with the next chunk's select of 1.17 ahead of it; DVE's score multiply stands behind an instruction that the addition stretches to 2.17. Without the chain and the norm (e3) the loop is at 18.7: so even there it is not shorter. The gain that the scan's parts do bring, 8.5 us in the two stretches, comes for the most part from the token-major sum (6.9, e10). No copy and no transposes stand between `inside` and the norm any more, and PE's wait for the normed `Y` of chunk 0 is 0.69 in e3; that this is how the sum gains is a reading of the trace. The prediction had that wait fall too, by a shorter loop, which did not come.

**What held.** The steps at 0.2 us alone and one to each POOL instruction beside it, and the forecast that the state stage would lose time. POOL's even count held roughly: an addition of 2.4 for a multiply of 1.90. The logarithm and its tables show no cost that can be told from zero (e10, 1.6 us below before with both in it). "What would show it" listed a multiply of output weights that waits at the head of DVE as what would prove it wrong; it is what happened.
